# Projections that may pass one another, weight loads in pieces of 512 columns into any free buffer, output row blocks that advance together

## The chip, the cores and the metric

The kernel runs on one core of one Trainium2 chip. The metric is the device time of one execution, in microseconds (us); several executions of the same program are timed and their median is taken. A profile is one further execution, taken by the hardware profiler.

## The reference, cut to what matters

Two layers of a hybrid decoder over 512 tokens of width 1024, all in float32. Each layer makes one wide input projection, runs three groups of attention heads on slices of it, multiplies each head group by a gate, projects back and normalises.

```python
def hybrid_layer(x, w_in, ..., w_out, ln_g, ln_b, layer_idx):
    h = jnp.einsum('bsd,de->bse', x, w_in)
    (dq, dk, dv, sq, sk, sv, iq, ik, iw, fq, fk, fv, ff, gate) = split_columns(h)
    ...
    a = diff_attention(dq, dk, dv, lam, pos)              # 4 heads, two softmax maps each
    ...
    bo = dsa_attention(sq, sk, sv, iq, ik, iw * IDX_WEIGHT_SCALE, pos, topk)   # index scores pick 128 keys
    ...
    co = forgetting_attention(fq, fk, fv, logf, pos)      # logits + cumulative log forget gate
    mixed = jnp.concatenate([a, bo, co], axis=-1) * jax.nn.silu(gate.astype(jnp.float32))
    out = jnp.einsum('bse,ed->bsd', mixed.astype(x.dtype), w_out)
    return layer_norm(DEEPNORM_ALPHA * x + out, ln_g, ln_b)
```

## The kernel before, in words

**Arithmetic.** Every float32 matrix is split into a high and a low part that TensorE takes directly: `whi`/`wlo` for weights, `xh`/`xl` for the activations. A product is three matmuls: high by high, low by high, high by low. `split` does this: ScalarE (ACT) copies the high part, and the subtraction that gives the low part goes to VectorE (DVE) or GpSimd (POOL), by `either`, which takes the one that would end first in the planner's account.

**Weights.** A `Weights` block is what one projection needs: 1024 columns for each partition (128 output columns by 8 slices of the inner dimension). `prep` loads it with one DMA on the SP queue into a `raw` buffer (two of them, 1024 columns each), and splits it into `whi` and `wlo` (four buffers each, used in turn). `prefetch(upto)` prepares blocks in their fixed order, up to three ahead of the projection that starts. `prep_out` does the same for the output weights; those of the second column half (`n` = 1) go into `qk` and `pt` buffers.

**The work on TensorE (PE).** Projections of queries, keys and gates are `w<-xh,whi`, `w<-xl,whi`, `w<-xh,wlo` (512 or 384 columns); projections of values are `w<-whi,xh` and its like (256 or 332 columns), and the output projection of `n` = 0 has the same names with 512 columns, or `w<-whi,pt` for the two head groups whose mixed rows lie in `pt` buffers. `w<-qk` are scores, `w<-cst,p` transposes of probabilities, `w<-cst,a` transposes of a finished diff head, `w<-vv,pt`, `w<-pt,vv` and `w<-pt,vd` products of probabilities and values. `w` is a ring of eight PSUM banks that all of them share.

**The order.** The program is written as generators (tasks) with priorities. A small planner, `Flow`, runs them against its own account of engine times: a task yields what it waits for (a bank, a buffer, an event, a time), the first ready task by priority goes on, and each engine's instructions are then emitted in the order of the times so planned. On the chip every engine takes its instructions strictly in that order.

- `attention` (priority of scores) walks the units `UNITS`; after the first it makes the index scores (`index_scores`): 4 query tiles by 3 row blocks, each a pair of 2 banks, read by ACT (relu) and then by a DVE accumulation into `acc`. Then `topk` runs in the gaps of DVE.
- `forget` makes the cumulative gate: on DVE it ends in two instructions `ccq<-tg,cst` (64x512) and two `cc<-tg,cst` (128x512).
- `later_projections` (priority of filling) makes the projections one after the other in the order of `plan`. A projection that needs `qk` or `vv` buffers waits for them, and everything behind it waits too.
- `output` does four row blocks (128 tokens each) for each column half `n`. For `n` = 0: rows 0 and 1 together in the order `EORDER` of the head groups, then row 2, then row 3, one after the other, each in the order 0 to 7.

Of the kernel before, what the change touches and what calls it, by code (L numbers as in the profile page):

```python
# [40 lines left out]
RINGS = {"qk": 14, "tg": 7, "p": 4, "pt": 6, "vv": 4, "a": 2}  # L41
SLACK = 1000
TOPK_SPAN = 112500
# [7 lines left out]
RAW, WHI, WLO = 2, 4, 4  # L51
# [244 lines left out]
def tile_hybrid_decoder(  # L296
# [174 lines left out]
    def load_x():  # L471
        yield "take", "pt", NB
        tiles, at = [], {}
        for k in range(KT):
# [7 lines left out]
            if k % 2 == 0:  # L482
                prefetch(k // 2)
# [9 lines left out]
    class Weights:  # L493


        def __init__(self, at, segs, ks, early):
            self.at, self.segs, self.ks, self.early = at, segs, ks, early
            self.m = sum(n for _, n in segs)
            self.n = len(ks) * self.m

        def prep(self):
            raw, hi, lo = [tile_of([KT * 128], tag, bufs, dt)[:, :self.n].rearrange("p (k c) -> p k c", k=len(self.ks))
                           for tag, bufs, dt in (("raw", RAW, F32), ("whi", WHI, F32R), ("wlo", WLO, F32R))]
# [3 lines left out]
            parts = len(self.ks) if self.at == 0 else 1  # L507
            for part in range(parts):
                c = slice(part, part + 1) if parts > 1 else slice(0, len(self.ks))
                dma(raw[:, c], src[:, c])  # L510
                ready = split(hi[:, c], lo[:, c], raw[:, c], 0 if self.early else PREP_BIAS)
                self.high = flow.ev["high"] if part == 0 else self.high
                for i, k in list(enumerate(self.ks))[c]:
                    self.hi[k], self.lo[k], self.ready[k] = hi[:, i], lo[:, i], ready

    def prep_out(l, n, e2):
        low = tile_of([KT, 128], "pt", 0, F32R) if n else tile_of([KT, 128], "wlo", WLO, F32R)
        lo = low.rearrange("p (e a) c -> p e (a c)", e=2)
        raw = tile_of([KT, 128], "raw", RAW).rearrange("p (e a) c -> p e (a c)", e=2)
        dma(raw, w_out[l, e2 * 256:(e2 + 1) * 256, n * 512:(n + 1) * 512]  # L520
            .rearrange("(e p) c -> p e c", p=128))
        if n:
            hi = [t512("qk", F32R) for _ in range(2)]
            ready = max(split(hi[e], lo[:, e], raw[:, e]) for e in range(2))
        else:
            hi = tile_of([KT, 128], "whi", WHI, F32R).rearrange("p (e a) c -> p e (a c)", e=2)
            ready = split(hi, lo, raw)
            hi = [hi[:, e] for e in range(2)]
        pieces[l, n, e2] = hi, [lo[:, e] for e in range(2)], ready, low
# [12 lines left out]
    first.append(len(groups))  # L542
    prepared = {"n": 0}
    pieces = {}

    def prefetch(upto, l=0):
        end = first[l + 1]
        while prepared["n"] <= min(upto, end - 1):
            groups[prepared["n"]].prep()
            prepared["n"] += 1  # L550
        for e2 in list(dict.fromkeys(e // 2 for e in EORDER))[:max(0, upto - end + 1)]:
            if (l, 0, e2) not in pieces:
                prep_out(l, 0, e2)

    def columns(l, w, pp, a, b):
        for t in range(a // 128, b // 128):
            yield "ev", ("xT", l, t)
        yield "at", max(w.ready.values())
# [7 lines left out]
    def proj(l, nm, j):  # L566
# [3 lines left out]
        if not soon:  # L570
            prefetch(g + AHEAD, l)
        yield "bank", "proj", 1
        pp = bank("proj")
        if soon:
# [3 lines left out]
            prefetch(g + WHI, l)  # L578
        else:
            yield from columns(l, w, pp, FIRST.get(nm, 0), S)  # L580
        return pp
# [67 lines left out]
    def v_group(l, nm, j):  # L649
# [5 lines left out]
        prefetch(g + AHEAD, l)  # L655
# [5 lines left out]
        for b0 in range(0, NB, nb):  # L661
            yield "bank", "proj", 1
            pp = bank("proj")
            for b in range(b0, b0 + nb):
# [3 lines left out]
                for w in ws:  # L668
                    yield "at", max(w.ready.values())
# [21 lines left out]
            flow.unbank("proj", pp)  # L691
        e = 128 if nm == "dv" else 64
# [660 lines left out]
```

## Time and profile before

| | before |
|---|---|
| median of 3 runs | 626.74 us (626.51 to 626.82) |
| the profiled execution, its own time | 627.08 us |
| span of its instructions | 625.1 us |
| mean granted TensorE clock | 0.993 |
| PE busy | 600.2 us, 96% of the span |
| DVE busy | 526.6 us, 84% |
| ACT busy | 392.6 us, 63% |
| POOL busy | 204.2 us, 33% |
| DMA engines, mean busy share | 38% |

The span reaches from the first to the last instruction; the time of an execution has 2.0 us around it here. Busy time counts an engine while at least one of its instructions runs. Matmuls are pipelined: a 512-column matmul shows 0.39 us from start to end, but in an unbroken run one starts every 0.23 us.

### The profile page before, as it was taken

Reading aid. Unit: us, or ns where it says so; the run is one execution under the profiler, and the core shown is the slowest. Engines: PE = TensorE matmul, PEld = TensorE weight load, DVE = VectorE, ACT = ScalarE, POOL = GpSimd, SP = SyncE. Lnnn points to the kernel's source line nnn. Section 1 sums busy time; section 2 is a strip of 40 time slices with the busy share of each in tenths; the row PEclk is TensorE's granted clock in tenths of the full one; section 3 lists DMA queues with packets and bytes.
Section 4 is the critical chain, followed back from the end, with each engine's and each line's share of the span. In section 5 each row is a group of like instructions: output and inputs, shape, how many; then the busy total and the mean of one; then the engine's idle time right before and its main releaser. Section 6 shows DMA issues by size and latency. Waiting matters only on the chain.

```text
span 625.1 us, 10304 instructions
## 1 busy us (share of the span) xinstructions
PE 600.2 (96%) x3385; PEld 523.4 (84%) x3385; DVE 526.6 (84%) x1299; ACT 392.6 (63%) x954; POOL 204.2 (33%) x179
## 2 busy tenths in 40 slices
PE   9999989999999999999999999999999999999994
PEld 7899879888888878778799988988898788888884
DVE  4689999998999987776857889999989999787666
ACT  5557866866676679933324667694955858987310
POOL 0016310466758800010001332034686694101000
PEclk9999989999999999999999999999999999999998
DMA  9564341334343522426136352324243343125402
GB/s 327 135 185 132 95 112 53 84 102 106 83 150 102 145 75 82 155 84 219 68 103 162 121 164 81 103 68 117 59 128 92 111 119 118 63 78 183 150 34 102
DMA packets 32198, 72.68 MB, mean 116 GB/s; under 512 B 5393, under 2 KB 6929, under 8 KB 32145
## 3 DMA queue, kind: packets, MB, share of 16 engines
q1 hardware_dynamic: 32144, 72.02, 38.4%
q8 instruction: 27, 0.44, 0.3%
q14 instruction: 27, 0.21, 0.1%
HBM read 53.13 MB, written 4.19 MB: 92 GB/s over the span
## 4 chain that ended last, share of the span: by engine, by line
PE 62%; DVE 14%; DMA 8%; ACT 5%; issue 4%; SPq 3%; POOL 3%; POOLq 0%; DVEq 0%; ACTq 0%
PE w L373 58%; DMA raw<-in_w_packed_dram 5%; PE w L376 3%; SPq L368 3%; DVE tg L351 2%; DVE acc L351 2%; DVE wlo L351 2%; DVE qk L351 1%; ACT whi L343 1%; DMA tg<-tg 1%; POOL lt L363 1%; ACT p L343 1%; DVE p L351 1%; DVE ccq L351 1%; POOL tg L363 1%
## 5 line engine op out<-in xcount | busy, mean ns | idle before, releaser
L373 PE MATMUL w<-xh,whi 128*128 128x512 f32 (+2 forms) x456 | 177.6, 391 | 1.9 <-DVE acc L351 0.6
L373 PE MATMUL w<-xh,wlo 128*128 128x512 f32 (+2 forms) x456 | 170.2, 374 | 0.0
L373 PE MATMUL w<-xl,whi 128*128 128x512 f32 (+2 forms) x456 | 169.7, 373 | 0.0
L363 POOL TENSOR_TENSOR wlo<-raw,whi 128x1024 fp32r<-128x1024 f32 x32 | 77.5, 2427 | 95.8 <-ACT whi L343 81.5
L343 ACT ACTIVATE whi<-raw 128x1024 fp32r<-128x1024 f32 (+3 forms) x77 | 80.0, 1039 | 32.2 <-DMA raw<-in_w_packed_dram 30.0
L373 PEld LDWEIGHTS w<-xh,whi 128*128 128x128 f32 x456 | 86.6, 190 | 14.1 <-DVE acc L351 1.1
L373 PEld LDWEIGHTS w<-xh,wlo 128*128 128x128 f32 x456 | 86.1, 189 | 14.5
L373 PEld LDWEIGHTS w<-xl,whi 128*128 128x128 f32 x456 | 86.6, 190 | 10.0
L373 PE MATMUL w<-qk 128*128 128x256 f32 (+3 forms) x352 | 72.7, 329 | 5.1 <-DVE acc L351 2.9
L373 PE MATMUL w<-whi,xh 128*128 128x256 f32 (+2 forms) x240 | 75.6, 315 | 1.1 <-ACT p L343 0.6
L373 PE MATMUL w<-whi,xl 128*128 128x256 f32 (+2 forms) x240 | 75.1, 313 | 0.2 <-DVE xl L351 0.2
L373 PE MATMUL w<-wlo,xh 128*128 128x256 f32 (+2 forms) x240 | 75.1, 313 | 0.0
L351 DVE TENSOR_TENSOR wlo<-raw,whi 128x1024 fp32r<-128x1024 f32 (+3 forms) x45 | 54.8, 1222 | 21.5 <-ACT whi L343 21.4
L343 ACT ACTIVATE p<-w,negm 128x128 f32<-128x128 f32 (+3 forms) x96 | 49.9, 525 | 32.7 <-DVE negm L351 32.3
L373 PEld LDWEIGHTS w<-qk 128*128 128x128 f32 x352 | 56.5, 189 | 12.7 <-DVE acc L351 4.2
L351 DVE MAX8 m<-acc 128x8 f32<-128x512 f32 (+2 forms) x96 | 52.8, 551 | 0.2
L351 DVE MATCH_REPLACE8 acc<-m,acc 128x384 f32<-128x384 f32 (+2 forms) x96 | 52.1, 543 | 0.0
L351 DVE CUSTOM_DVE_ANT_0 w<-w,cst 128x128 f32<-128x128 f32 (+3 forms) x104 | 47.3, 494 | 5.5 <-PE w L373 5.3
L343 ACT ACTIVATE qk<-tg 64x512 fp32r<-64x512 f32 (+1 forms) x60 | 36.0, 600 | 20.6 <-POOL tg L363 12.6
L373 PEld LDWEIGHTS w<-whi,xh 128*128 128x128 f32 x240 | 45.4, 189 | 3.7 <-ACT xh L343 0.9
L373 PEld LDWEIGHTS w<-whi,xl 128*128 128x128 f32 x240 | 45.5, 189 | 3.2 <-DVE xl L351 1.0
L351 DVE TENSOR_TENSOR pt<-w,pt 128x128 fp32r<-128x128 f32 (+3 forms) x96 | 44.5, 483 | 3.2 <-ACT pt L343 2.5
(132 smaller groups left out, 1132.0 us busy)
## 6 DMA issues: line engine op xcount, KB each, us to landing
raw<-in_w_packed_dram SPq DMA_DIRECT2D x61, 512.0 KB, 3.8
raw<-in_w_out_dram SPq DMA_DIRECT2D x16, 512.0 KB, 3.4
qk<-qk SPq DMA_DIRECT2D x56, 128.0 KB, 2.3
tg<-tg SPq DMA_DIRECT2D x88, 64.0 KB, 2.0
pt<-in_xT_dram SPq DMA_DIRECT2D x8, 256.0 KB, 5.6
raw<-in_w_packed_dram SPq DMA_DIRECT2D x4, 498.0 KB, 4.5
tg<-tg SPq DMA_DIRECT2D x32, 48.0 KB, 2.5
vv<-in_ln_g_dram SPq DMA_DIRECT2D x2, 512.0 KB, 5.7
```

What stands on the lines that cost most here:

```text
L343: lambda: nc.scalar.activation(o, i, func, **kw))
L351: lambda: getattr(nc.vector, name)(o, *args, **kw), port=two_ports(name, o, ins))
L363: lambda: getattr(nc.gpsimd, name)(o, *args, **kw), port=name != "memset")
L368: return flow.issue("sp", 640 if ins else 475, outs, ins, lambda: nc.sync.dma_start(o, i), width(o) * o.shape[0] * 4)
L373: lambda: nc.tensor.matmul(o, lhsT, rhs, **kw))
L376: flow.issue("pe", 109.0, [o], [i, ident], lambda: nc.tensor.transpose(o, i, ident))
```

## The change

- Weight buffers `whi` and `wlo` become a free list: a projection gives its pair back when its last matmul is planned (`used`), and `fill` starts the next block in line at once. `prefetch` is gone.
- A block is loaded and split in pieces of 512 columns (of one 332-column slice for the first value block), through four `raw` buffers of 512 columns in place of two of 1024.
- `later_projections` takes the first projection in line whose buffers are free and whose weights are ready; if none is, it waits for the first. A rope step that lacks its `tg` buffers is left to a task of its own.
- The row blocks of the output projection's first half become three tasks (`out_rows`), all in the order `EORDER`.

```diff
-RINGS = {"qk": 14, "tg": 7, "p": 4, "pt": 6, "vv": 4, "a": 2}
+RINGS = {"qk": 14, "tg": 7, "p": 4, "pt": 6, "vv": 4, "a": 2, "whi": 4, "wlo": 4}
+READY = 500
+WAITING = 1
-RAW, WHI, WLO = 2, 4, 4
+RAW = 4
...
         def prep(self):
-            raw, hi, lo = [tile_of([KT * 128], tag, bufs, dt)[:, :self.n].rearrange("p (k c) -> p k c", k=len(self.ks))
-                           for tag, bufs, dt in (("raw", RAW, F32), ("whi", WHI, F32R), ("wlo", WLO, F32R))]
+            self.slots = slot("whi"), slot("wlo")
+            hi, lo = [u[:, :self.n].rearrange("p (k c) -> p k c", k=len(self.ks)) for u in self.slots]
...
-            parts = len(self.ks) if self.at == 0 else 1
-            for part in range(parts):
-                c = slice(part, part + 1) if parts > 1 else slice(0, len(self.ks))
-                dma(raw[:, c], src[:, c])
-                ready = split(hi[:, c], lo[:, c], raw[:, c], 0 if self.early else PREP_BIAS)
+            size = max(1, 512 // self.m) if self.at else 1
+            for k0 in range(0, len(self.ks), size):
+                c = slice(k0, min(k0 + size, len(self.ks)))
+                raw = tile_of([512], "raw", RAW)[:, :(c.stop - k0) * self.m].rearrange("p (k c) -> p k c", c=self.m)
+                dma(raw, src[:, c])
+                ready = split(hi[:, c], lo[:, c], raw, 0 if self.early else PREP_BIAS)
...
+    def unslot(slots):
+        for tag, u in zip(("whi", "wlo"), slots):
+            flow.give(tag, u)
+        fill()
...
+    def fill(most=4):
+
+        while most and blocks_to_come and flow.free["whi"] and flow.free["wlo"]:
+            blocks_to_come.pop(0)()
+            most -= 1
...
     def later_projections(l):
...
+        def can_go(nm, j):
+            tag, n = need(nm)
+            g = number[l, nm, j]
+            blocks = [w for w in groups[g:g + 3] if w.segs == groups[g].segs]
+            return sum(t <= flow.now for t in flow.free[tag]) >= n and \
+                all(w.ready and max(w.ready.values()) <= flow.now + READY for w in blocks)
+        while todo:
+            short = set()
+            for nm, j in todo:
+                if need(nm)[0] not in short or not need(nm)[1]:
+                    if can_go(nm, j):
+                        break
+                    short.add(need(nm)[0])
+            else:
+                nm, j = todo[0]
...
     def output(l):
...
+        def out_rows(n, rows, ys):
+            yield "bank", "proj", len(rows)
+            pp = {t: bank("proj") for t in rows}
+            end = l + 1 == DEPTH and rows[-1] == NB - 1
+            for cs in (slice(0, 256), slice(256, 512)) if n and end else (slice(0, 512),):
+                for c, e in enumerate(range(8) if n else EORDER):
+                    yield "ev", (l, "m", e)
...
-            for rows in ((0, 1), (2,), (3,)) if n == 0 else ((0,), (1,), (2,), (3,)):
-                tag = "s" if n == 0 and rows[0] == 2 else "proj"
...
+            groups_of_rows = ((0, 1), (2,), (3,)) if n == 0 else ((0,), (1,), (2,), (3,))
+            for rows in groups_of_rows:
+                if n == 0:
+                    flow.add(PRIO_S, out_rows(n, rows, ys))
+                else:
+                    yield from out_rows(n, rows, ys)
```

What the change does to the order, at three places. The first is PE in layer 0, at the index scores (`w<-qk` with 256, 384 and 512 columns, four matmuls for a pair of banks). Before, the second of the four rounds stands so, with a transpose and six projection matmuls in it:

```order
L373 MATMUL w<-qk 128x256 x4
L373 MATMUL w<-xh,whi 128x512
L373 MATMUL w<-xl,whi 128x512
L373 MATMUL w<-xh,wlo 128x512
L373 MATMUL w<-qk 128x384 x4
L376 MATMUL w<-cst,a 128x128 x4
L373 MATMUL w<-xh,whi 128x512
L373 MATMUL w<-xl,whi 128x512
L373 MATMUL w<-xh,wlo 128x512
L373 MATMUL w<-qk 128x512 x4
```

In the change the second round has matmuls of a value projection (256 columns) ahead of its last pair, and behind it, up to the third round's first pair:

```order
L375 MATMUL w<-qk 128x256 x4
L375 MATMUL w<-qk 128x384 x4
L375 MATMUL w<-whi,xh 128x256
L375 MATMUL w<-whi,xl 128x256
L375 MATMUL w<-wlo,xh 128x256
...
L375 MATMUL w<-qk 128x512 x4
L375 MATMUL w<-whi,xh 128x256
L375 MATMUL w<-whi,xl 128x256
...
L375 MATMUL w<-qk 128x256 x4
```

Twelve value matmuls stand at the first dots (with the three shown) and 36 between the 512 pair and the next 256 pair, so a value projection has passed projections that stood ahead of it in the line. The change also has one place, from the third round into the fourth, where three pairs follow each other with nothing between them.

The second place is DVE in the same stretch. Before, both `ccq` instructions stand right behind the first round's accumulations, and the whole second round follows:

```order
L351 SCALAR_TENSOR_TENSOR acc_186<-w,wi,cst 128x512
L351 SCALAR_TENSOR_TENSOR acc_186<-w,wi,acc_186 128x512
L351 SCALAR_TENSOR_TENSOR ccq_74<-tg,cst 64x512
L351 SCALAR_TENSOR_TENSOR ccq_75<-tg,cst 64x512
L351 SCALAR_TENSOR_TENSOR acc_184<-w,wi,acc_184 128x256 x2
L351 TENSOR_TENSOR tg<-w,cst 128x384
```

In the change they stand in the second round, with only its 512 accumulations behind them:

```order
L353 SCALAR_TENSOR_TENSOR acc_209<-w,wi,acc_209 128x256 x2
L353 SCALAR_TENSOR_TENSOR acc_210<-w,wi,acc_210 128x384 x2
L353 SCALAR_TENSOR_TENSOR ccq_74<-tg,cst 64x512
L353 SCALAR_TENSOR_TENSOR ccq_75<-tg,cst 64x512
L353 SCALAR_TENSOR_TENSOR acc_211<-w,wi,acc_211 128x512 x2
L353 TENSOR_TENSOR vv<-w,vv 128x2x128 x2
```

They have moved behind four index accumulations, and what follows them reads the 512 pair, behind which PE now has the 36 value matmuls.

The third place is DVE at the end of layer 0, where the last unit's probabilities are split into `pt` (`pt<-w,pt`, 128x4x128) for the last product with the values. Before, that split stands behind a gate (`tg`, `m`), four splits of mixed rows (`xl`) and a whole weight block:

```order
L351 TENSOR_TENSOR pt<-m_248,pt 128x512
L351 TENSOR_TENSOR pt<-m_343,pt 128x512
L351 SCALAR_TENSOR_TENSOR tg<-tg,w 128x512
L351 TENSOR_TENSOR m_743<-m_743,tg 128x512
...
L351 TENSOR_TENSOR xl<-m_736,xh 128x512
L351 TENSOR_TENSOR wlo<-raw,whi 128x1024
L351 TENSOR_TENSOR pt<-w,pt 128x4x128 x2
L351 SCALAR_TENSOR_TENSOR junk<-w,junk 64x256 x2
L351 TENSOR_TENSOR xl<-m_119,xh 128x512
```

In the change it stands right behind the two splits of mixed rows:

```order
L353 TENSOR_TENSOR pt<-m_281,pt 128x512
L353 TENSOR_TENSOR pt<-m_385,pt 128x512
L353 TENSOR_TENSOR pt<-w,pt 128x4x128 x2
L353 TENSOR_TENSOR wlo<-raw,whi 128x512 x2
L353 SCALAR_TENSOR_TENSOR tg<-tg,w 128x512
L353 TENSOR_TENSOR m_773<-m_773,tg 128x512
```

The split has moved ahead of the weight block, the gate and the four `xl` splits. On PE the last product `w<-pt,vd` (14 matmuls) stands in the same place of the attention. Before, 12 matmuls of rows 0 and 1 follow it and then those of the last head group (`e` = 4), which need that product's result; in the change 42 matmuls (rows 0 and 1, and row 2) stand between the product and the first matmul of the last head group.

## Rows read from the trace of the kernel before

**Rows 1.** The page: busy time, share of the span and instructions of each engine.

```profile
PE 600.2 (96%) x3385; PEld 523.4 (84%) x3385; DVE 526.6 (84%) x1299; ACT 392.6 (63%) x954; POOL 204.2 (33%) x179
```

**Rows 2.** Busy time by stretch (PE, PEld, DVE, ACT, POOL, granted clock, DMA share, GB/s).

```profile
76.50:80.00 3.50, 0.59 (x4) 0.16 (x2) 3.35 (x4) 2.88 (x6) 3.50 (x2) 1.00 0.71 182
80.50:85.00 4.50, 4.50 (x14) 3.54 (x13) 4.30 (x8) 1.00 (x3) 0.00 (x0) 0.62 0.25 100
100.00:150.00 50.00, 50.00 (x281) 43.30 (x281) 47.42 (x141) 35.91 (x88) 22.14 (x12) 1.00 0.29 77
260.00:277.00 17.00, 14.83 (x68) 10.96 (x67) 12.51 (x18) 10.15 (x21) 3.47 (x3) 1.00 0.11 32
616.00:625.10 9.10, 0.17 (x2) 0.00 (x0) 5.10 (x14) 0.47 (x1) 0.54 (x1) 0.73 0.26 99
```

**Rows 3.** PE in order of time: start, us, instruction, idle before and its releaser.

```profile
76.40 0.62 PE L373 MATMUL w<-qk 128*128 128x512 f32 x2
79.93 0.73 PE L373 MATMUL w<-qk 128*128 128x512 f32 x2 [2.91 <-DVE acc L351]
```

**Rows 4.** The chain that ended last, two lines of it: start, us, what.

```profile
75.94 0.65 DVE ccq L351
76.61 2.75 DVE ccq L351
...
388.44 2.79 DVE ccq L351
```

**Rows 5.** POOL and DVE in order of time beside it.

```profile
75.95 2.86 POOL L363 TENSOR_TENSOR wlo<-raw,whi 128x1024 fp32r<-128x1024 f32 x1 [2.37 <-ACT whi L343]
...
79.39 1.07 DVE L351 SCALAR_TENSOR_TENSOR acc<-w,wi,acc 128x256 f32<-128x256 f32 x2
```

**Rows 6.** PE in order of time at the end of layer 0.

```profile
261.53 0.49 PE L373 MATMUL w<-whi,pt 128*128 128x512 f32 x1 [0.79 <-ACT pt L343]
...
265.69 0.50 PE L373 MATMUL w<-whi,xl 128*128 128x512 f32 x1 [0.18 <-DVE xl L351]
270.92 1.10 PE L373 MATMUL w<-pt,vd 128*128 128x256 f32 x7 [0.48 <-DVE pt L351]
275.24 0.50 PE L373 MATMUL w<-whi,xh 128*128 128x512 f32 x1 [0.48 <-ACT xh L343]
```

**Rows 7.** DVE in order of time at the end of layer 0.

```profile
264.95 2.49 DVE L351 TENSOR_TENSOR xl<-m,xh 128x512 fp32r<-128x512 f32 x4
267.36 2.31 DVE L351 TENSOR_TENSOR wlo<-raw,whi 128x1024 fp32r<-128x1024 f32 x1
269.59 1.28 DVE L351 TENSOR_TENSOR pt<-w,pt 128x512 fp32r<-128x512 f32 x2
```

**Rows 8.** Groups by shape: busy us, mean ns of one, idle before and its releasers.

```profile
L363 POOL TENSOR_TENSOR wlo<-raw,whi 128x1024 fp32r<-128x1024 f32 x32 | 77.5, 2427 | 95.8 <-ACT whi L343 81.5 <-issue 9.0 <-PE w L373 4.6
L351 DVE TENSOR_TENSOR wlo<-raw,whi 128x1024 fp32r<-128x1024 f32 x37 | 46.3, 1255 | 9.4 <-ACT whi L343 9.3
L343 ACT ACTIVATE whi<-raw 128x1024 fp32r<-128x1024 f32 x69 | 73.1, 1059 | 26.8 <-DMA raw<-in_w_packed_dram 26.4
L363 POOL TENSOR_TENSOR tg<-tg,cst 128x512 f32<-128x512 f32 x17 | 22.2, 1307 | 42.8 <-DMA tg<-tg 42.7
L351 DVE TENSOR_TENSOR pt<-raw,qk 128x512 fp32r<-128x512 f32 x16 | 10.2, 687 | 2.6 <-ACT qk L343 2.5
L343 ACT ACTIVATE qk<-raw 128x512 fp32r<-128x512 f32 x16 | 9.0, 620 | 9.3 <-DMA raw<-in_w_out_dram 9.3
```

**Rows 9.** DMA issues (count, KB each, us to landing), and their time on the SP queue (min/median/max ns).

```profile
raw<-in_w_packed_dram SPq DMA_DIRECT2D x61, 512.0 KB, 3.8
raw<-in_w_packed_dram SPq DMA_DIRECT2D x2, 256.0 KB, 3.2
...
L368 SPq DMA_DIRECT2D raw<-in_w_packed_dram x69: 327/436/583, 1.2 to 528.4; - x69
```

**Rows 10.** What PE waited for: us in total, times, longest us.

```profile
PE w L373 <- DVE acc L351: 3.5, 2, 2.9
```

More of the change, by code (lines that the diff above doesn't have):

```diff
@@ new lines, in prep, with used, slot @@
+            flow.set(("prepared", self.at), flow.now)
+        def used(self):
+            unslot(self.slots)
+    def slot(tag):
+        t = min(flow.free[tag])
+        flow.free[tag].remove(t)
+        u = tile_of([KT * 128], tag, 0, F32R)
+        flow.born[u.tensor.name] = t
+        return u
+    def unslot(slots):
+        for tag, u in zip(("whi", "wlo"), slots):
+            flow.give(tag, u)
+        fill()
+    def prep_out(l, n, e2):
+        slots = [tile_of([KT * 128], "pt", 0, F32R)] if n else [slot("whi"), slot("wlo")]
+        lo = slots[-1].rearrange("p (e c) -> p e c", e=2)
+        hi, ready = [], 0
+        for e in range(2):
+            raw = tile_of([512], "raw", RAW)
+            at = e2 * 256 + e * 128
+            dma(raw, w_out[l, at:at + 128, n * 512:(n + 1) * 512])
+            hi.append(t512("qk", F32R) if n else slots[0].rearrange("p (e c) -> p e c", e=2)[:, e])
+            ready = max(ready, split(hi[e], lo[:, e], raw))
+        pieces[l, n, e2] = hi, [lo[:, e] for e in range(2)], ready, slots
+        flow.set((l, "w", n, e2), flow.now)
@@ L541, in tile_hybrid_decoder @@
             at += 128 * groups[-1].n
-    first.append(len(groups))
-    prepared = {"n": 0}
     pieces = {}
[L546 to L553, printed above, removed]
+    blocks_to_come = []
+    for l in range(DEPTH):
+        blocks_to_come += [g.prep for g in groups[first[l]:(first + [None])[l + 1]]]
+        blocks_to_come += [lambda l=l, e2=e2: prep_out(l, 0, e2) for e2 in dict.fromkeys(e // 2 for e in EORDER)]
+    def fill(most=4):
+        while most and blocks_to_come and flow.free["whi"] and flow.free["wlo"]:
+            blocks_to_come.pop(0)()
+            most -= 1
     def columns(l, w, pp, a, b):
@@ L691, in v_group @@
             flow.unbank("proj", pp)
+        for w in ws:
+            w.used()
         e = 128 if nm == "dv" else 64
@@ L1147, in later_projections, with need @@
             yield "ev", (l, "early", nm, j)
-        for nm, j in order[l][len(early(l)):]:
-            if nm in ("dq", "dk", "sq", "iq"):
-                yield from rope_group(l, nm, j)
+        todo = order[l][len(early(l)):]
+        def need(nm):
+            return ("vv", 2) if nm in ("dv", "fv") else ("qk", SLOTS.get(nm, 0))
+        def can_go(nm, j):
[13 more added lines that the diff above has]
+                nm, j = todo[0]
+            if nm in ("dq", "dk", "sq", "iq"):
+                yield "take", "qk", SLOTS[nm]
+                pp = yield from proj(l, nm, j)
+                if sum(t <= flow.now for t in flow.free["tg"]) < 2 and waiting[0] < WAITING:
+                    flow.add(PRIO_POST, rope_later(l, nm, j, pp))
+                else:
+                    yield from rope(l, nm, j, pp)
             elif nm in ("fq", "fk"):
```

110 lines of the change are left out of this document (48 added, 62 removed).

## The prediction

> **What bounds the kernel now.** I read the page first: PE is busy for 600.2 us of a span of 625.1 [rows 1], every other engine for less. The change removes no matmul, so it can only take from the 24.9 us in which PE is idle, and from time in which PE runs slowly. The table by stretch tells where these lie. From 616.0 on PE has done its work (0.17 us busy of 9.1) and the last normalisation ends the program: 8.9 us that the change leaves as they are [rows 2]. The first 1.5 us are start-up. So some 14.5 us of idle time lie in the middle, and two stretches hold a third of it.
>
> *The index scores of layer 0.* Between 76.5 and 80.0 PE is busy for 0.59 us of 3.5 [rows 2]. PE's own order shows two of four score matmuls at 76.40 and the other two at 79.93, after 2.91 us in which it waited for DVE's `acc` [rows 3]. Why DVE was late is in the chain that ended last: one `ccq` takes 0.65 us, the next of the same shape 2.75 [rows 4]. A POOL subtraction of a whole weight block (`wlo`, 1024 columns) runs beside it, 2.86 us from 75.95, so it ends at 78.81; the `ccq` ends at 79.36, 0.55 later, about one `ccq` long, and at 79.39 DVE can at last read the scores [rows 5]. So DVE waited out the POOL instruction: 2.75 - 0.65 = 2.1 us. The wait has a tail: from 80.5 to 85.0 the granted clock averages 0.62 of 2.4 GHz, after 1.00 in the stretch before [rows 2], so for most of it PE ran at the lower level (1.2 GHz), and 4.5 x 0.38 = 1.7 us are lost. The place costs 2.9 + 1.7 = 4.6 us.
>
> *The end of layer 0.* From 260 to 277 PE is busy for 14.83 of 17 us at full clock [rows 2]: 2.2 us idle. Five waits make it up, 0.79 the first and 0.48 the last [rows 6]. The first matmul after a wait shows 0.50 us, where one in an unbroken run shows 0.39, so each costs some 0.1 us more: about 2.7 us. The fourth waits for DVE's split `pt`, which started at 269.59 because four `xl` of 2.49 us and a `wlo` of 2.31 us stood ahead of it on DVE [rows 7]; a DVE `wlo` takes 1.25 us in the mean [rows 8]. The fifth waits for the mixed rows of the last head group.
>
> The other 14.5 - 2.9 - 2.2 = 9.4 us are short waits in many places.
>
> **The change, part by part.**
>
> *Projections that pass.* In the first place the second round's last pair now has 12 value matmuls ahead of it and 36 behind it before the next pair. Seven matmuls of 256 columns take 1.10 us, pipelined start included [rows 6], so 36 are between 4 and 5.7 us: more than the 2.1 us by which one POOL block held DVE. And the two `ccq` now stand so that the accumulations behind them free banks that PE wants only after those 36. Bounds: nothing gained, if the wait only moves to another round (a rival below), and 4.6 us, if it is gone. I take 4.2, near the upper bound, because the cover is longer than the hold-up; 0.4 is left for a short wait.
>
> *Pieces of 512 columns.* Each piece of POOL's subtraction holds DVE no longer than its own length. The nearest row is a POOL product of 512 columns, 1.31 us against 2.43 for 1024 [rows 8]; the worst hold-up falls from 2.4 to 1.3 us. What the pieces cost: the order has DVE subtract 83 pieces of 512 and 16 of 332 columns, for 37 of 1024 and eight smaller before; POOL 57 of 512, for 32 of 1024. By the busy time of a group divided by its count a DVE subtraction of 512 is 10.2 / 16 = 0.64 us and one of 1024 is 46.3 / 37 = 1.25; ACT's copy 9.0 / 16 = 0.56 and 73.1 / 69 = 1.06 [rows 8]. With 0.48 us for 332 columns (between 0 and 0.64) DVE goes from about 55 to 83 x 0.64 + 16 x 0.48 = 61 us, 6 us more; ACT from 80 to 140 x 0.56 + 16 x 0.47 = 86, also 6 more; POOL from 77.5 to 57 x 1.31 = 75. None of it is on PE's path as long as DVE has room, and the hardest stretch says that it has: from 100 to 150 DVE is busy for 47.4 of 50 us, and PE for all 50 [rows 2]. Five rope and query steps of DVE go to POOL in the change, which at 0.64 us each takes 3 of the 6 us back. I count zero; if the cover is gone, at most the 6 us of DVE.
>
> *More transfers.* 85 loads of weights become 172, half as long. A load of 512 KB lands after 3.8 us, one of 256 KB after 3.2, and an issue takes 0.44 us on the SP queue [rows 9]: 87 x 0.44 = 38 us more on SP over the whole program, ahead of the rope and key copies that are queued there too. A piece's way is 3.2 + 0.62 + 1.31 = 5.1 us with POOL [rows 8, 9], and four are under way: two pieces each 2.6 us. A block's way was 3.8 + 1.06 + 2.43 = 7.3 us with two under way: one each 3.6 us. A projection uses a block in 24 matmuls, over 5 us. So the loads keep ahead in both, and the larger number is hidden: zero. The Trainium skill ("DMA: Bandwidth & Descriptors", section "Bandwidth") speaks against the pieces: transfers should be batched to 1 MiB or more, because about 2 us of each are fixed. By that figure 87 more transfers would be 174 us of fixed time, an estimate, and not hidden if they ran one after another; the rows say instead that a half-size load lands only 0.6 us sooner, which is the same observation, and that several are under way at once.
>
> *Any free buffer.* Blocks are started earlier. PE's longest wait is for `acc` (3.5 us in two waits, the longest 2.9 [rows 10]), the others of the two places for `pt`, `xl` and `xh` [rows 6], none for `whi` or `wlo`. Nothing, either way.
>
> *Row blocks together.* At the end of layer 0 the split `pt` moves ahead of a gate and of 2.49 + 2.31 us of `xl` and `wlo` work on DVE [rows 7], and 42 matmuls (some 9.5 us) stand where 12 stood between the last product and the group that needs it. So the fourth and fifth wait, 2 x 0.6, should go, and six projection matmuls stand ahead of the first wait, where none did. Bounds 0 and 2.7; I take 2.2.
>
> **The sum.** 4.2 + 2.2 = 6.4 us off the profiled execution's 627.08, so 620.7. The median of the runs lies 0.34 us lower, so **620.3 us**.
>
> **The rivals.**
>
> *The other short waits shrink too.* The planner now has more work to choose from at each wait, in both layers, and every POOL hold-up is halved. For it: the second layer has a `ccq` of 2.79 us as well [rows 4]. Against it: PE's second wait for `acc` is 0.6 us at most (3.5 less 2.9 [rows 10]), and nothing in the rows says that the 9.4 us are of one kind. If half of them go: 620.3 - 4.7 = 615.6.
>
> *The pieces use up the gain.* Issues on SP may stand in the way of the copies that keys and ropes wait for: of the 38 us of additional issues a sixth on PE's path is 6.4, the whole gain. Then the time is about 626.7, no change. It is what the Trainium skill's rule on batching ("DMA: Bandwidth & Descriptors", section "Bandwidth") would lead one to expect. For it: SP is one queue, and it takes the pieces in twos to eights between the copies. Against it: PE waited for no copy at the two places.
>
> *Slower: the wait moves to where three index pairs now follow each other with nothing between.* They need six of eight banks at once; each bank comes back only when DVE has accumulated. If DVE is behind there by the 2.9 us seen before, in both layers, each place costs 4.6 with the clock's fall: 4.6 x 2, less the old 4.6 and the 2.2 of the layer's end, is 2.4 us more than now: 629.1. It decides when a wait reaches the length at which the clock fell: 2.9 us did it, 0.79 at 261.5 did not [rows 2, 3, 6]. For it: DVE is about as full as before in that stretch. Against it: the pairs stand behind 16 value matmuls, and what held DVE up is halved.
>
> **How the numbers follow.** The forecast has 0.50 and a range of its own from 617 to 624 (the two places kept at 3 to all of their 7.3, and some short waits either way). More gain, around 615.6, has 0.20; the gain used up, around 626.7, 0.12; slower, around 629, 0.18. A difference under 0.2% (1.25 us) can't be told from none in this kernel. Faster than that: 0.50 + 0.20 + a little of the third, 0.72; the same 0.10; slower 0.18. For 8 in 10 the range runs from 613.5, which cuts the far end of the larger gain, to 628.0, which holds the no-change case and cuts most of the slower one.
>
> **What would show it.** PE's idle time falls from 24.9 to about 20 us, with the same 9 us at the end. In the index scores of layer 0 no wait of PE for `acc` reaches 1 us and the clock stays at 1.00; no `ccq` is over 2 us. At the end of layer 0 no wait for `pt` or `xh` stands between the last `w<-pt,vd` and the first matmul of the last head group. DVE's and ACT's busy time rise by some 3 and 6 us. The prediction is wrong if PE's idle time is spread over new waits of the same sum: for `acc` in a later round, or for copies that SP issued late.

## The result, and the profile after

The changed kernel takes 612.13 us (611.67 to 612.43), the kernel before beside it 626.62 (626.39 to 626.82): a ratio of 0.9767 [0.9751, 0.9783], 14.5 us less. The direction was forecast; the size was not, and the time lies below the range. The profiled execution has a span of 610.1 us, 15.0 less, at the same mean clock of 0.993.

The page of after, to be read beside [rows 1]:

```profile
PE 595.8 (98%) x3385; PEld 524.5 (86%) x3385; DVE 525.2 (86%) x1348; ACT 403.0 (66%) x1033; POOL 203.8 (33%) x209
```

What PE waited for in it (us in total, times, longest us):

```profile
PE w L375 <- ACT p L345: 1.9, 1, 1.9
PE w L375 <- DVE junk L353: 1.5, 1, 1.5
PE w L378 <- ACT p L345: 1.3, 3, 0.7
PE w L378 <- DVE p L353: 0.7, 2, 0.4
```

PE is idle for 610.1 - 595.8 = 14.3 us, 24.9 before. 8.9 of them are the end and 1.5 the start (`junk`), as before, so 3.9 stay in the middle, in the other six waits. There were 14.5, nearly all in 22 waits of that view; the longest beside [rows 10], and the one on PE itself, were

```profile
PE w L373 <- DVE pt L351: 2.3, 4, 1.1
PE w L373 <- DMA qk<-qk: 1.2, 2, 0.9
PE w L376 <- DVE tg L351: 1.1, 2, 0.6
PE w L376 <- ACT p L343: 1.0, 1, 1.0
...
PE w L373 <- PE w L373: 0.4, 1, 0.4
```

Busy time by stretch, to be read beside [rows 2] (PE, PEld, DVE, ACT, POOL, granted clock, DMA share, GB/s):

```profile
72.00:90.00 18.00, 18.00 (x134) 17.31 (x133) 17.20 (x31) 14.23 (x34) 5.02 (x5) 1.00 0.29 97
160.50:165.00 4.50, 4.50 (x27) 4.50 (x26) 4.29 (x15) 2.06 (x8) 3.40 (x3) 0.62 0.01 2
245.00:262.00 17.00, 17.00 (x100) 14.55 (x99) 13.77 (x32) 16.43 (x40) 1.24 (x1) 1.00 0.54 169
367.00:385.00 18.00, 18.00 (x131) 17.18 (x130) 16.96 (x31) 15.12 (x35) 3.63 (x4) 1.00 0.32 100
600.00:610.10 10.10, 1.25 (x11) 1.05 (x9) 6.14 (x15) 0.47 (x1) 0.54 (x1) 0.75 0.27 104
```

PE never stops in the index scores of layer 0 (72 to 90) and of layer 1 (367 to 385), nor at the end of layer 0 (245 to 262), and the clock there is 1.00. DVE's two `ccq`, to be read beside [rows 4], now take 1.50 us as a pair:

```profile
84.59 1.50 DVE L353 SCALAR_TENSOR_TENSOR ccq<-tg,cst 64x512 fp32r<-64x512 f32 x2
...
372.03 1.50 DVE L353 SCALAR_TENSOR_TENSOR ccq<-tg,cst 64x512 fp32r<-64x512 f32 x2
```

The groups of the pieces, to be read beside [rows 8]; a piece of 256 KB lands after 3.2 us, as the two did that were there before [rows 9]:

```profile
L345 ACT ACTIVATE whi<-raw 128x512 fp32r<-128x512 f32 x140 | 83.2, 627 | 29.5 <-DMA raw<-in_w_packed_dram 24.6 <-PE w L375 4.0
L365 POOL TENSOR_TENSOR wlo<-raw,whi 128x512 fp32r<-128x512 f32 x57 | 72.9, 1297 | 112.0 <-ACT whi L345 91.2 <-PE w L378 11.0 <-PE w L375 4.3
L353 DVE TENSOR_TENSOR wlo<-raw,whi 128x512 fp32r<-128x512 f32 x83 | 56.0, 708 | 7.2 <-ACT whi L345 6.8
```

One long wait is left, where PE in order of time shows

```profile
159.94 0.38 PE L375 MATMUL w<-whi,xh 128*128 128x256 f32 x1 [1.90 <-ACT p L345]
```

and ACT beside it

```profile
158.02 1.28 ACT L345 ACTIVATE qk<-tg 64x512 fp32r<-64x512 f32 x2 [2.64 <-POOL tg L365]
159.32 0.47 ACT L345 ACTIVATE p<-w,negm 128x256 f32<-128x256 f32 x1
```

ACT stands for 2.64 us at the head of a rope step that POOL computes, and the probabilities `p` that would free PE's bank are queued behind it. After that wait the clock averages 0.62 from 160.5 to 165, so most of that stretch ran at the lower level: 4.5 x 0.38 = 1.7 us more, as much as the fall at 80.5 cost before.

**Where the 15.0 us came from.** Idle time fell by 24.9 - 14.3 = 10.6 us and busy time by 600.2 - 595.8 = 4.4. Busy time falls although no matmul is gone: in an unbroken run a matmul of 512 columns overlaps the next by 0.39 - 0.23 = 0.16 us, which a wait loses, and the first matmul after it shows 0.1 more (0.49 at 261.53 [rows 6]). 22 - 6 = 16 waits fewer, at 0.26 each, are 4.2, an estimate from these rows; the lower clock cost 1.7 in one place before and 1.7 in another after, so it cancels.

To compare places in kernels with different orders, I give each matmul the usual distance to the next start of its shape (0.227 us for 512 columns, 0.119 for 256, and so on); that sums to 574.6 us in every kernel. What the trace runs beyond this sum, up to PE's last matmul, is delay: waits, lost overlap and lower clock together. The other kernels are those of the experiments below. The delay is that of one profiled execution, and that lies up to 3.7 us off the median beside it (608.5 us for loads and copies in pieces, 632.1 for free buffers and pieces, 622.6 for values early). The table gives it by the work done so far (so that a row means the same place), and the value matmuls that the order has from the first to the last of the twelve index pairs, in layer 0 and layer 1 (a value projection has 96).

| kernel | median us | delay | 50-100: index scores, layer 0 | 225-275: end of layer 0 | 350-400: index scores, layer 1 | 500-575: end of layer 1 | value matmuls |
|---|---|---|---|---|---|---|---|
| before | 626.6 | 41.6 | 6.6 | 4.6 | 2.9 | 1.1 | 48, 72 |
| after | 612.1 | 26.6 | 1.2 | 0.8 | 1.7 | 1.9 | 96, 96 |
| after, nudged | 612.1 | 27.0 | 1.6 | 1.9 | 2.3 | 2.2 | 96, 96 |
| after, nudged back | 613.5 | 28.3 | 0.8 | 6.7 | 1.9 | 1.1 | 96, 96 |
| before, nudged | 623.6 | 37.1 | 5.3 | 5.0 | 2.8 | 1.3 | 48, 72 |
| no passing | 621.2 | 36.2 | 5.0 | 4.2 | 3.2 | 1.7 | 48, 60 |
| no passing, nudged | 614.2 | 27.5 | 3.5 | 0.6 | 3.2 | 1.5 | 48, 48 |
| whole blocks | 619.0 | 33.3 | 6.6 | 0.6 | 3.5 | 1.2 | 24, 96 |
| whole blocks, nudged | 616.9 | 31.0 | 2.8 | 1.1 | 5.4 | 1.3 | 96, 96 |
| rows apart | 617.5 | 32.5 | 1.2 | 3.0 | 1.8 | 5.2 | 96, 96 |
| free buffers alone | 634.4 | 48.4 | 6.3 | 11.0 | 0.9 | 2.2 | 36, 60 |
| free buffers and pieces | 629.1 | 46.8 | 5.4 | 9.5 | 3.0 | 6.4 | 48, 60 |
| loads and copies in pieces (whole subtraction) | 612.2 | 23.2 | 2.4 | 0.5 | 3.0 | 1.1 | 96, 96 |
| copies in pieces | 627.9 | 41.6 | 8.6 | 0.4 | 6.7 | 0.8 | 0, 0 |
| loads in pieces | 628.2 | 43.0 | 7.0 | 5.1 | 5.8 | 1.2 | 24, 24 |
| split subtraction | 628.6 | 44.5 | 9.9 | 1.7 | 9.8 | 1.2 | 0, 0 |
| split subtraction, nudged | 631.6 | 45.0 | 10.0 | 2.6 | 5.3 | 1.3 | 0, 96 |
| values do not pass | 629.7 | 45.1 | 4.4 | 9.1 | 7.5 | 2.1 | 60, 12 |
| copies in pieces, values early | 619.8 | 36.9 | 1.2 | 3.1 | 2.2 | 1.1 | 96, 96 |

By it 15.0 us of delay went: 5.4 in the first place (6.6 to 1.2), 3.8 in the second (4.6 to 0.8), and 5.8 elsewhere. Between the two places layer 0 got worse by 2.6 (7.4 to 10.0 at 100 to 225, which holds the wait at 159.94); layer 1 gave 8.0, of which 5.0 at 400 to 500.

### The profile page after: what moved, and what is told of

Read it like the earlier page. It is cut to its first block, busy times and chain, and to the rows that moved or that the text cites. A ratio compares the mean times of both kernels' runs of the same rounds, so it can differ in the third digit from the quotient of the medians.

```text
span 610.1 us, 10685 instructions
## 1 busy us (share of the span) xinstructions
PE 595.8 (98%) x3385; PEld 524.5 (86%) x3385; DVE 525.2 (86%) x1348; ACT 403.0 (66%) x1033; POOL 203.8 (33%) x209
## 2 busy tenths in 40 slices
DMA packets 42681, 72.71 MB, mean 119 GB/s; under 512 B 6784, under 2 KB 10368, under 8 KB 42624
## 3 DMA queue, kind: packets, MB, share of 16 engines
q1 hardware_dynamic: 42624, 72.03, 38.9%
## 4 chain that ended last, share of the span: by engine, by line
PE 84%; DVE 8%; ACT 4%; issue 1%; POOL 1%; DMA 1%; SPq 0%; POOLq 0%; DVEq 0%; ACTq 0%
PE w L375 79%; PE w L378 5%; DVE acc L353 2%; ACT p L345 2%; DVE m L353 1%; DVE qk L353 1%; DVE p L353 1%; DMA raw<-in_w_packed_dram 1%; DVE tg L353 1%; DVE wlo L353 1%; DVE w L353 1%; ACT w L345 0%; ACT whi L345 0%; SPq L370 0%; ACT qk L345 0%
## 5 line engine op out<-in xcount | busy, mean ns | idle before, releaser
L345 ACT ACTIVATE whi<-raw 128x512 fp32r<-128x512 f32 (+1 forms) x156 | 90.3, 612 | 40.7 <-DMA raw<-in_w_packed_dram 33.1
L365 POOL TENSOR_TENSOR wlo<-raw,whi 128x512 fp32r<-128x512 f32 x57 | 72.9, 1297 | 112.0 <-ACT whi L345 91.2
L375 PEld LDWEIGHTS w<-xh,wlo 128*128 128x128 f32 x456 | 85.8, 188 | 14.3
L353 DVE TENSOR_TENSOR wlo<-raw,whi 128x512 fp32r<-128x512 f32 (+1 forms) x99 | 63.3, 675 | 14.7 <-ACT whi L345 14.2
L365 POOL TENSOR_TENSOR tg<-tg,cst 128x512 f32<-128x512 f32 (+1 forms) x24 | 30.4, 1267 | 65.5 <-DMA tg<-tg 65.3
L353 DVE MATCH_REPLACE8 acc<-m,acc 128x512 f32<-128x512 f32 (+2 forms) x96 | 52.0, 542 | 0.0
L375 PEld LDWEIGHTS w<-wlo,xh 128*128 128x128 f32 x240 | 46.1, 192 | 1.8
```

The lines of the kernel that those rows point to most:

```text
L345: lambda: nc.scalar.activation(o, i, func, **kw))
L353: lambda: getattr(nc.vector, name)(o, *args, **kw), port=two_ports(name, o, ins))
L365: lambda: getattr(nc.gpsimd, name)(o, *args, **kw), port=name != "memset")
L375: lambda: nc.tensor.matmul(o, lhsT, rhs, **kw))
```

## The experiments

**One part undone.** Each kernel is the changed one with one part put back.

Without passing (nor ropes that wait in a task of their own):

```diff
-                    if can_go(nm, j):
+                    if (nm, j) == todo[0]:
...
-                if sum(t <= flow.now for t in flow.free["tg"]) < 2 and waiting[0] < WAITING:
+                if False:
```

With whole blocks:

```diff
-RAW = 4
+RAW = 2
...
-            size = max(1, 512 // self.m) if self.at else 1
+            size = len(self.ks) if self.at else 1
...
```

With rows apart, as before the change:

```diff
-                for c, e in enumerate(range(8) if n else EORDER):
+                for c, e in enumerate(range(8) if n or rows[0] else EORDER):
...
-                if n == 0:
-                    flow.add(PRIO_S, out_rows(n, rows, ys))
-                else:
-                    yield from out_rows(n, rows, ys)
+                yield from out_rows(n, rows, ys)
```

> The changed kernel with the projections again in their fixed order (and the rope step never put off); free weight buffers, pieces of 512 columns and joint row blocks stay. If the gain lies in the two places that I named, passing is worth about 4.6 us of the 14.5 and this runs at about 616.7. If passing gives PE other work at most of the short waits, it is worth 9 us or more, and this runs at 621 or above. If the pieces or the free buffers do it, this stays under 614.

> The changed kernel with weight blocks loaded and split whole again (two raw buffers of 1024 columns, one copy and one subtraction for a block); passing, free buffers and joint row blocks stay. If pieces cost nothing and give nothing, 612. If the shorter hold-up of DVE by POOL is what removed the short waits all over the program, they come back: 4.7 to 9 us, so 617 to 621. If the pieces cost engine time that shows, under 611.

> The changed kernel with the first half of the output projection row block by row block again, in its old order; the rest stays. By the prediction 2.2 us of the gain are here, at the end of layer 0: 614.3. If the other parts had removed those waits already, 612. The second layer's end had no waits before, so more than 615 would mean something else.

Measured: without passing 621.16 us (0.992 [0.9892, 0.9949] of before), with whole blocks 618.98 (0.9885 [0.986, 0.9911]), with rows apart 617.49 (0.9869 [0.9833, 0.9904]). So each part was worth something in this order: 9.0, 6.9 and 5.4 us. Pieces, which I had at zero, were not nothing, and rows together gained more than twice what I gave it in this order. Where it did is plain, since the two orders have nearly the same delay elsewhere; PE with the rows apart, at the end of layer 0 and of layer 1:

```profile
264.12 0.50 PE L375 MATMUL w<-whi,xl 128*128 128x512 f32 x1 [1.12 <-DVE xl L353]
270.37 0.50 PE L375 MATMUL w<-whi,xl 128*128 128x512 f32 x1 [0.47 <-DVE xl L353]
570.82 0.50 PE L375 MATMUL w<-whi,xh 128*128 128x512 f32 x1 [0.98 <-ACT xh L345]
572.51 0.50 PE L375 MATMUL w<-whi,xl 128*128 128x512 f32 x1 [0.96 <-DVE xl L353]
```

In layer 0 that is 3.0 - 0.8 = 2.2 us of delay, the term of my sum; in layer 1 another 5.2 - 1.9 = 3.3, at a place where the kernel before had waited little (1.1).

**Parts alone, on the free buffers.**

> Of the change only the free list of weight buffers and the earlier start of blocks: projections in fixed order, whole blocks, rows apart. By the prediction this part gives nothing: 626.6, the same as before. If blocks that start earlier are what the planner needed, 618 to 622.

> The kernel of e4 once more, whose profile was taken in a disturbed execution: 634.4. Its trace should show where 8 us over the kernel before go. If blocks that start earlier crowd the SP queue, PE waits for copies of keys and ropes; if it is the changed order of engines' work, the waits are for DVE and ACT.

> Free buffers and pieces of 512 columns; projections in fixed order and rows apart. If the parts add up, undoing passing and rows together costs 9.0 + 5.4 us: 626.5. If free buffers cost something only with whole blocks, which fill the queue and the engines in larger lumps, under 624. If the pieces help only a kernel that passes projections, 631 or more.

The three parts undone at once (both runs are one kernel; the table has the second) give 634.42 us (633.56 to 635.07), 1.0123 [1.0106, 1.014] of before: the free list by itself loses 8. With pieces it is 629.06, 1.0039 [1.0026, 1.0051]. PE with free buffers alone, at the end of layer 0:

```profile
263.87 0.50 PE L375 MATMUL w<-whi,pt 128*128 128x512 f32 x1 [1.65 <-ACT pt L345]
267.66 1.22 PE L375 MATMUL w<-whi,pt 128*128 128x512 f32 x2 [3.06 <-DVE pt L353]
```

Behind the 3.06 us the clock shows 0.50 from 267 to 272. PE's waits for copies of keys are 1.7 us in all there, so the SP queue is not what loses. Rows together, added to the kernel with pieces, gain 629.1 - 621.2 = 7.9, again at the two ends of layers (9.5 to 4.2, and 6.4 to 1.7; the profile with pieces is one of 632.1 us).

**Which piece?** I held that a shorter POOL subtraction holds DVE less. One kernel loads and copies in pieces but subtracts a block at once:

```diff
...
+                    flow.set("high", act(hi[:, c], raw))
+                    if c.stop < len(self.ks):
+                        continue
+                    c, raw = slice(0, len(self.ks)), whole
+                    ready = either(lo, raw, hi.bitcast(F32), OP.subtract, 0 if self.early else PREP_BIAS)
...
```

Another loads and copies whole and splits only the subtraction:

```diff
...
+                    flow.set("high", act(hi, raw))
...
+                        ready = either(lo[:, d], raw[:, d], hi[:, d].bitcast(F32), OP.subtract, 0 if self.early else PREP_BIAS)
...
```

> The changed kernel with loads and copies in pieces of 512 columns, but one subtraction of 1024 columns for a block (on DVE or POOL), raw buffers of 1024. If the pieces help because a POOL subtraction of 1024 columns holds DVE up for 2.4 us, this loses what e2 lost: 619. If they help because a block's parts arrive and are copied sooner, it stays near 612 to 614.

> The changed kernel with whole loads and whole copies of 1024 columns, but the subtraction in pieces of 512. If the hold-up of DVE by POOL is what counts, 612 to 613. If the arrival of parts counts, 619 as in e2.

The whole subtraction gives 612.16 us (608.47 to 614.47; 0.9763 [0.9724, 0.9802]), as good as the change; the split one 628.59 (1.0039 [1.0023, 1.0054] of before). So the shorter hold-up by POOL is not what gains. PE with the split subtraction, in the index scores of layer 0:

```profile
76.19 0.51 PE L375 MATMUL w<-qk 128*128 128x256 f32 x2 [1.24 <-DVE acc L353]
78.12 2.04 PE L375 MATMUL w<-qk 128*128 128x256 f32 x6 [1.42 <-DVE tg L353]
84.18 0.50 PE L375 MATMUL w<-xh,whi 128*128 128x512 f32 x1 [1.88 <-ACT m L345]
```

**How much is the order's luck?** The planner's cost of a matmul, 1 ns higher or lower, alters the order here and there and nothing else.

```diff
-        flow.issue("pe", width(o) / 2.262 + 2, [o], [lhsT, rhs],
+        flow.issue("pe", width(o) / 2.262 + 3, [o], [lhsT, rhs],
```

> The changed kernel, with the planner's account of a matmul 1 ns longer (width / 2.262 + 3 in place of + 2). Nothing is computed otherwise, but near-ties in the plan fall differently and the order changes on every engine. If the gains of the parts are the parts' own, this runs within 2 us of 612.1. If a part's gain is mostly the luck of one order, it moves by as much as the parts do: 5 to 9 us.

> The same with 1 ns less (+ 1). Within 2 us of 612.1 if the order's luck is small; 617 or more, or under 608, if it is as large as the parts.

> The kernel before, with the planner's account of a matmul 1 ns longer. Within 2 us of 626.4 if the order's luck is small; off by 5 us or more either way if not, and then the wait of 2.9 us in the index scores, of which I made most of the forecast, need not be there.

> The kernel of e2 (whole blocks) with the same nudge of 1 ns. Near 619 if the 6.9 us of the pieces are their own; near 612 if e2 was an unlucky order.

> The run with whole loads and copies and the subtraction in pieces (628.6) with the planner's cost of a matmul 1 ns higher, which alters the order here and there and nothing else. If 628.6 is what split subtractions do: 626 to 631. If it was an unlucky order over what whole blocks give (616.9 to 619.0): 615 to 622.

> The run without passing (621.2) with the planner's cost of a matmul 1 ns higher. If the 9 us that passing was worth are its own: 619 to 623. If a good part was the order: 613 to 618, or above 625.

The change gives 612.11 and 613.46 us, the kernel before 623.61 (0.9951 [0.9926, 0.9976]), whole blocks 616.89, the split subtraction 631.60, no passing 614.23 (612.61 to 615.22) in place of 621.16. So the whole change stands well outside this scatter, but the price of a single part does not: passing is worth 9.0 us in one order and 2.1 (614.23 - 612.11) in the other, pieces 6.9 and 4.8. The whole change is worth 14.5 and, with both kernels nudged, 623.61 - 612.11 = 11.5.

Two places show it. The wait for `acc` in the kernel before is still there when it is nudged, a little shorter, but the clock doesn't fall behind it (PE, and the stretch behind it; both to be read beside [rows 2, 3]):

```profile
79.97 0.73 PE L373 MATMUL w<-qk 128*128 128x512 f32 x2 [2.37 <-DVE acc L351]
80.50:85.00 4.50, 4.50 (x21) 3.70 (x20) 4.30 (x9) 1.00 (x3) 0.00 (x0) 1.00 0.27 107
```

And the changed kernel nudged back has a delay of 6.7 us at the end of layer 0, where it has 0.8 as it is; PE there, and the stretch behind it, with a clock of 0.50:

```profile
254.76 1.12 PE L378 MATMUL w<-cst,p 128*128 128x128 f32 x4 [2.07 <-ACT p L345]
255.00:260.00 5.00, 4.98 (x14) 3.67 (x14) 4.06 (x7) 5.00 (x11) 0.22 (x1) 0.50 0.21 67
```

**Loads alone, copies alone** (on the kernel with a whole subtraction). Copies in pieces:

```diff
...
+                if self.at and k0 == 0:
+                    dma(whole, src)
...
```

Loads in pieces, with one copy behind the last:

```diff
...
+                    flow.set("high", act(hi, whole))
...
```

> The changed kernel with each weight block loaded by one transfer of 1024 columns and subtracted in one, so that only ACT's copy is in pieces of 512. Theory 1 (a copy of 1024 columns holds ACT for 1.06 us, one of 512 for 0.56, and steps that PE waits for stand behind it): about 612, as with copies and loads in pieces (612.2). Theory 2 (it is the load: a half block lands and is worked on sooner, and a half-size raw buffer is not what matters): about 619, as with whole blocks (619.0, nudged 616.9). Theory 3 (neither, but the order that the planner happens to find): anything from 611 to 622, not in line with the next run.

> The counterpart of the last: each weight block loaded in pieces of 512 columns, copied by one instruction of 1024 and subtracted by one of 1024. Theory 1 (ACT's long copies cost the time): about 619. Theory 2 (the loads in pieces gain the time): about 612. Theory 3 (the order found): not in line with the last run; for instance both near 612 or both near 619.

627.92 us (1.003 [1.0014, 1.0046]) and 628.21 (1.0038 [1.0017, 1.0058]): neither is near 612 nor near 619, where the kernel with both and the kernel with none are. A price of one piece can't explain that, so the third theory is left, and the table says what in the order differs: value matmuls among the index pairs. With 96 of them the index scores cost 0.8 to 5.4 us of delay in the table, with 24 or fewer 5.8 to 10.0, with numbers between anything from 0.9 to 6.6. So the count keeps the two ends apart, but it does not set the delay by itself. PE with copies in pieces, in layer 0 (two rows) and layer 1:

```profile
77.46 1.14 PE L375 MATMUL w<-qk 128*128 128x384 f32 x4 [1.09 <-DVE tg L353]
81.11 2.08 PE L375 MATMUL w<-qk 128*128 128x512 f32 x4 [2.51 <-DVE acc L353]
383.75 1.65 PE L375 MATMUL w<-qk 128*128 128x512 f32 x3 [2.52 <-DVE acc L353]
```

The stretch behind the first two:

```profile
80.00:90.00 10.00, 8.88 (x30) 7.14 (x31) 9.31 (x17) 7.02 (x15) 2.37 (x1) 0.66 0.01 2
```

PE waits for the accumulations, as before, but without a `ccq` held by POOL; DVE is simply behind (9.31 of 10 us). What value projections do there can be read from the groups of after:

```profile
L353 DVE TENSOR_TENSOR vv<-w,vv 128x256 fp32r<-128x256 f32 x16 | 6.0, 412 | 0.0
```

One value projection is 96 matmuls of 0.119 us, 11.4 us of PE, and asks DVE for four such subtractions, 1.6 us. That leaves DVE time to accumulate. Whether other work between the pairs would do as well isn't shown: counted in the same way, the orders with 96 value matmuls have 106 to 129 matmuls of all kinds other than scores there, those with 24 or fewer 28 to 58.

**One rule for value projections changed, both ways.** Nothing else is edited, though the planner then finds another order in other places too. On the changed kernel, values do not pass:

```diff
-                    if can_go(nm, j):
+                    if can_go(nm, j) and (nm not in ("dv", "fv") or (nm, j) == todo[0]):
```

On copies in pieces, values early:

```diff
-                all(w.ready and max(w.ready.values()) <= flow.now + READY for w in blocks)
+                all(w.ready and max(w.ready.values()) <= flow.now + (1500 if nm in ("dv", "fv") else READY) for w in blocks)
```

> The changed kernel (612.1) in which every projection may pass except a value projection, which goes when it is first in line. Its order has 24 value matmuls among the index pairs of layer 0, all of them late, where the changed kernel has 108, and 12 in layer 1 where that has 132. Theory 1 (what gains is that value projections, which ask little of DVE, stand between the index pairs): PE waits for acc and tg again in both layers' index scores, and the time is between 619 and 628, with most of the difference in these two stretches. Theory 2 (the gain is passing as such, or loads that come sooner): about 612 to 615, no wait over 1 us in the index scores.

> The run with copies alone in pieces (627.9), and one number changed: a value projection may be taken when its weights are to be ready within 1500 ns, not 500. Its order then has 96 value matmuls between the index pairs in each layer, where it had none among them. Theory 1: the waits of 1.3 and 2.7 us for acc in the index scores of both layers go, and the time falls by 8 to 12 us, to 616 to 620. Theory 2 (value projections are not it): the time stays at 625 to 630.

(Counted from the first to the last pair, the value matmuls are 60 and 12 in the first of these, and 96 and 96 in the changed kernel; the text of the expectation had other numbers.) If values do not pass, 629.67 us (628.02 to 630.59; 1.0049 [1.0033, 1.0065] of before): the whole gain is lost, more than I expected. If they come early, copies in pieces fall from 627.92 to 619.75 (618.31 to 622.57; 0.9886 [0.9862, 0.9909]). Both moved as the first theory says, the first of them beyond the 628 that it gave. PE with values that do not pass, at the index scores of layer 1 (two rows) and at the end of layer 0:

```profile
384.76 2.07 PE L375 MATMUL w<-qk 128*128 128x512 f32 x4 [1.48 <-DVE acc L353]
388.04 0.80 PE L375 MATMUL w<-xh,whi 128*128 128x512 f32 x1 [1.21 <-ACT m L345]
262.71 0.80 PE L375 MATMUL w<-whi,pt 128*128 128x512 f32 x1 [3.65 <-ACT pt L345]
```

In layer 0 the waits among the index pairs are short, 0.53 us the longest. The stretch behind the first two rows:

```profile
385.00:395.00 10.00, 8.68 (x29) 6.37 (x29) 9.41 (x17) 6.40 (x14) 0.00 (x0) 0.66 0.00 0
```

Of its 18.5 us of delay more than after, 9.0 are in the two index stretches (3.2 and 5.8), not most as expected, and 8.3 at the end of layer 0: taking the values away from one place also makes another order there. With values early, the stretches of the index scores run through:

```profile
70.00:80.00 10.00, 10.00 (x64) 9.05 (x63) 8.65 (x15) 8.21 (x20) 3.60 (x4) 1.00 0.40 107
80.00:90.00 10.00, 10.00 (x79) 9.81 (x78) 9.44 (x16) 7.97 (x18) 2.42 (x1) 1.00 0.28 92
385.00:395.00 10.00, 10.00 (x74) 9.64 (x73) 9.50 (x18) 6.64 (x17) 0.74 (x1) 1.00 0.15 53
```

but the wait for copies of keys or queries, 1.5 us in all with copies in pieces, now stands first among PE's:

```profile
PE w L375 <- DMA qk<-qk: 3.4, 5, 1.5
```

The index stretches give 7.4 + 4.5 = 11.9 us of delay back, and 7.2 are lost again elsewhere, 3.4 - 1.5 = 1.9 of them in waits for copies: 4.7 net by the two profiles, 8.2 by the medians.

No version beat the changed kernel: the one with a whole subtraction ties with it.

## Why the prediction was right in direction and wrong in size

- **The first place: right in cause, and nearly in size.** 4.2 us forecast, 5.4 of delay gone (3.7 with both kernels nudged); `acc` is no longer waited for, no `ccq` is over 2 us, the clock stays at 1.00. But I put it down to passing alone, and compared the cover with one POOL hold-up. The 1.7 us for the clock belonged to that order: nudged, the kernel before waits 2.37 us there at a clock of 1.00. What the runs showed is broader: with value matmuls ahead of and between the pairs the index scores lose less, in both layers, whether or not POOL holds DVE. Passing brings them there if the planner counts their weights as ready: letting them go 1.0 us earlier brought all 96 into both layers. That the pieces act by this is argued; whole blocks have 24 of them in layer 0 in one order and 96 in the other.
- **The second place: near in size, less sure in cause.** 2.2 forecast, 3.8 of delay gone; with the rows apart 2.2 come back. That these two figures agree is luck: with rows together the place has 0.4 to 9.1 us of delay in the table (6.7 in the changed kernel nudged back, where PE waits for `p`), with rows apart 3.0 to 11.0. In the two pairs that differ in the rows alone, rows together help there (3.0 to 0.8, and 9.5 to 4.2), but other things in the order weigh as much. That the same edit would gain 3.3 at the end of layer 1 was missed: before there was no such wait to see in [rows 6] or elsewhere, and it appears only when the rest is faster.
- **Pieces: the zero failed.** I priced them by DVE's busy time and by POOL's hold-up. Undone they cost 4.8 to 6.9 us, and the hold-up is not the reason. Whole blocks lose all of theirs in the two index stretches (5.4 + 1.8 us of delay), and of the kernels that keep a part of the pieces, those with copies or a split subtraction lose 12.4 of 15.0 and 16.8 of 17.9 there, with 0 value matmuls, the one with loads 9.9 of 16.4.
- **More transfers: right.** The issues doubled, the time of the packets went from 38.4% to 38.9% of the engines' span with 42681 packets for 32198, and PE waits for no weight block. The rule of the Trainium skill ("DMA: Bandwidth & Descriptors", section "Bandwidth") to batch transfers to 1 MiB or more does not show as a cost here: half-size loads land after 3.2 us for 3.8 [rows 9], and several are under way. (The 2 us of the prediction stand in another section of that page, for transfers issued from GpSimd; these are issued from SP.)
- **Any free buffer: "nothing, either way" failed.** Alone it loses 8 us, most of it at the end of layer 0 (11.0 for 4.6). Why the planner's order gets worse there stays open.
- **The step that failed most** is "the other 14.5 - 2.9 - 2.2 = 9.4 us are short waits in many places", which I left as they were. They fell to 3.9 us, and with the overlap lost at each wait that is 5.8 of delay gone, more than either place. A part of that is luck of the old order: with both kernels nudged the same rest is 10.1 - 3.7 - 3.1 = 3.3. I had this as a rival at 4.7 and gave it 0.20, because nothing in the rows said that the waits were of one kind. By the view of waits they were of one kind: all but 1.2 us for copies and a little for PE itself were for DVE or ACT (18 of the 22). That each was late because of what stood ahead in that engine's queue is argued; it was followed up at 159.94 and at the places above, not one by one. I also priced a wait at its idle time plus 0.1; by the rows above it is some 0.26 more than its idle time, which is one reason why the two places were priced too low as well, by 1.2 and 1.6 us of delay.
- **Engines.** ACT rose by 10.4 us where 6 were forecast: a copy of 512 columns took 83.2 / 140 = 0.59 us, not 0.56, one of 332 0.44, and there are 156. DVE fell by 1.4 where I forecast a rise of 3: the four `ccq` alone went from 7.0 us of busy time to 3.0.
- **The slower rival** did not occur in the change. Three pairs in a row stand there without a wait. But it is what the kernel with copies in pieces, at 628 us, shows: pairs close together, waits of 1.1 and 2.5 us, and a clock of 0.66 behind them.

## What to carry to other kernels

Where a scheduler gets more choice, don't stop at the named stalls: here the short waits elsewhere gave as much as either of them. More choice is no gain by itself: the free list alone lost 8 us. Ask of the short waits what queue each stands in, and add the lost overlap to each. In this kernel a stretch in which one engine feeds another in pairs wanted work between the pairs that asks little of the late engine, and whether such work came there decided more than the cost of any single instruction. Before a part of a change to a scheduler is given a price, repeat it with the order nudged: kernels with a part undone moved by up to 7 us here, the kernel before by 3.0, the changed kernel by 1.4 at most.

## What was not expected of the hardware

A wait of 1.90 us was followed by a mean clock of 0.62 (160.5 to 165 in after), so mostly the lower level of 1.2 GHz, where 2.91 us was the shortest wait of which I had seen it [rows 2, 3]; two waits of 1.09 and 2.51 us 3.6 us apart are followed by 0.66 over ten microseconds. With whole blocks a wait of 1.55 us at 386.55 was followed by a clock of 1.00, and in the kernel before, nudged, one of 2.37 us was too, while 2.07 us in the changed kernel, nudged back, was followed by 0.50. So in these traces the length of the wait alone does not tell whether the clock falls, as the prediction's slower rival took it to.
